# A decoder layer on one core: the residual's moves over six tiles by token half, and the sum with the second half in the later group

## The chip, the core and the metric

The kernel runs on one core of one Trainium2 chip. The metric is the device time of one launch in microseconds (us); lower is better. PE is TensorE, DVE is VectorE, ACT is ScalarE, POOL is GpSimd and SP is SyncE, whose queue issues most transfers. Each engine executes its own queue of instructions in the order in which the built program lists them. That order is not the order of the source: a scheduler in the tile framework sets it at build time, from estimates of its own, under the dependencies between instructions. One changed instruction can so move others, on several engines.

## The reference

One layer: a sparse attention and a causal pooling side by side, a residual and a layer norm, then a gated feed-forward part with a residual and a layer norm. Only the feed-forward part matters here:

```
h = layer_norm(ALPHA * h + mix, ln1_g, ln1_b)          # 272 tokens x 2048; 256 tokens are put out
z = h @ w_up                                           # 2048 -> 2 x 5632
z = sum(zp[:, j:j + T] * conv_w[j] for j in range(3)) + conv_b
a, g = split(z, 2)
f = (gelu(a) * g) @ w_down                             # 5632 -> 2048
h = layer_norm(ALPHA * h + f, ln2_g, ln2_b)
```

## The kernel before

All arithmetic is in float32, and each product is made of three matmuls: every operand is split into a high part (a reduced-precision float32 that PE takes at full rate) and the rest, the low part, and high x high, high x low and low x high are summed.

**Weight tiles.** Every weight tile has 128 x 2048 numbers, 1 MB. `fetch` loads it on SP's queue (L111). Then ScalarE makes the high part, in two cuts of the columns (L124), and VectorE the low part (L125); this is called the conversion below. Three raw tiles and three converted ones can be live at a time. A raw tile's place comes free when its conversion is done, a converted tile's when PE is done with it.

**The feed-forward plan.** `ffn_plan` lists the work by f, the number of a block of 128 inner columns, 0 to 43, in parts of 8. For each f there are two *up tiles*, first half (`za`) and second half (`z`), each of 48 matmuls (L175 to L177, `product`) followed by the convolution of its sum: one operation on ScalarE (L683), two on VectorE (L684, L685). After the second, `gate` does the activation (L700) and the product (L701). Pairs of f are then made into the operands of the down product by `forms`: sums on GpSimd (L720 to L723), splits on ScalarE and VectorE (L706, L707).

For the first four parts the down product is done by a scheme with seven products in place of eight. `seven` works a part's down tiles in two column halves c, and each half in two groups: group A has the products P2, P3, P1, P5 and four tiles, called A j=0 to 3, of 12 matmuls each; group B has P7, P6, P4 and four tiles of 9 matmuls (L745 to L747). The tiles of a part go between the up tiles of the next: up, A, up, A, and so on. The tiles of part 0 stand between the up tiles of f=8 to 15: A j=0 to 3 in f=8 and 9, B j=0 to 3 in f=10 and 11, then the second column half from f=12. Before their conversion the weights of an A tile need one subtraction (L116), those of a B tile three operations (L119 to L121), all on VectorE.

**The result y2.** `y2` holds the residual and the running sum: two token halves i=0 and 1 of 128 tokens, each with 2048 columns. For a column half c, c11 and c12 are pieces of 512 columns in token half 0, c21 and c22 the same in token half 1. At the end of group A ScalarE copies P1 and P5 out as u and v (L757, L759), and VectorE adds P2 to c11, P3 to c12 and v to c22 (`add`, L753). Accumulating transfers on GpSimd's queue then add u to c11 and v to c12 (L763, L764). At the end of group B VectorE makes u += P6 (L767) and v = u + P7 (L768) and adds P4 to c21, and three transfers (L770 to L772) add u to c12 and v to c21 and c22.

**The moves.** The residual enters y2 by 32 transfers on SP's queue (L677, `residual`), each of 32 partitions x 16 x 32 numbers, 64 KB in runs of 128 bytes, one for each of four source blocks a, four destination blocks b and two token halves i. The blocks in place are turned by VectorE at f=4 and 5 (L842). The list `moves` has i as its fastest index, and 8 moves go out after each of f=6, 7, 8 and 9, between the loads of weight tiles. An addition into y2 waits for the moves that write its piece, thus the first ones at the end of group A of f=9.

Of the kernel before, what the change touches and what calls it, by code (L numbers as in the profile page):

```python
# [36 lines left out]
FOLDED = 4  # L37
# [32 lines left out]
def tile_layer(ctx, tc, xt, w_first, w_proj, w_uk, w_uv, w_pool, w_o, w_up, w_down, cols, rows, rel_bias, onehot, out):  # L70
# [8 lines left out]
    def big():  # L79
        return pm.tile([P, 512], F32, tag="mm", name="mm")  # L80

    def small():
        return pa.tile([P, 512], F32, tag="at", name="at")
# [46 lines left out]
    def emit(i):  # L130
        if i in ready:
            return
        if i == last:

            raw = wp.tile([P, 2048], F32, tag="wraw", name="wraw")
            nc.sync.dma_start(raw, stream[i])
            ready[i] = []
            for c in range(0, 2048, 256):
                hl = ring.tile([P, 2, 256], F32R, tag="act", name="whl_r", padded_shape=[P, 2, T])
                nc.scalar.activation(hl[:, 0, :], raw[:, c:c + 256], AF.Copy)  # L140
                nc.vector.tensor_tensor(hl[:, 1, :], raw[:, c:c + 256], hl[:, 0, :].bitcast(F32), op=ALU.subtract)
                ready[i].append(hl)
            return
        if i == spare:
            raw = wp.tile([P, 2048], F32, tag="wraw", name="wraw")
            hl = sb.tile([P, 2, 2048], F32R, tag="y", name="whl_y")
        else:
            raw, hl = weight_tiles()
        fetch(raw, hl, stream[i], kinds.get(i))
        ready[i] = hl  # L150
# [6 lines left out]
    def weights(ahead=2):  # L157
        i = state["use"]
        state["use"] += 1
        prefetch(i + 1 + ahead)  # L160
        return ready.pop(i)
# [7 lines left out]
    def product(ps, hl, m, act, lo, hi, ks=range(KT), width=P, k0=0, k1=KT):  # L169

        for n in range(k0, k1):
            k = ks[n]
            wh, wl = hl[:, 0, k * width:k * width + m], hl[:, 1, k * width:k * width + m]
            ah, al = act[k][:, 0, lo:hi], act[k][:, 1, lo:hi]
            nc.tensor.matmul(ps, wh, ah, start=n == 0, stop=False)  # L175
            nc.tensor.matmul(ps, wh, al, start=False, stop=False)  # L176
            nc.tensor.matmul(ps, wl, ah, start=False, stop=n == KT - 1)  # L177
# [3 lines left out]
    for k0, k1 in [(k, k + 1) for k in range(9)] + [(9, 12), (12, 15), (15, 16)]:  # L181
# [7 lines left out]
        for k in range(k0, k1):  # L189
            xk, wk, c = raw[:, k % 3, :T], raw[:, k % 3, T:], slice(k % 6 * MF, k % 6 * MF + MF)  # L190
            a = ring.tile([P, 2, T], F32R, tag="act", name="xp")
# [84 lines left out]
    v = sb.tile([P, 3], F32, name="rms_v")  # L276
# [103 lines left out]
    for i, (a, b) in enumerate(((0, NM), (NM, NM + P), (NM + P, T))):  # L380
        if i:
            v = ap_.tile([b - a, 1024], F32, name=f"v{i}")
        else:

            v = ap_.tile([80, 1024], F32R, name="v0")
# [290 lines left out]
        to = y2[dst, i, :].rearrange("p (m d) -> p m d", d=P)[:, :, src]  # L676
        nc.sync.dma_start(to, y[src, :, t:t + 32])  # L677

    moves = [(a, b, i) for a in range(4) for b in range(4) for i in range(2)]

    def conv(j, half_, src, za):
        z = fp.tile([P, S], F32, name="z", tag="z1") if half_ else za
# [16 lines left out]
    def gate(za, zg):  # L699
        nc.scalar.activation(za, za, AF.Gelu_apprx_tanh)  # L700
        nc.vector.tensor_tensor(za, za, zg, op=ALU.mult)  # L701

    held = {}
# [30 lines left out]
    def seven(kind, part, c, j):  # L734

        hl = weights()
        n = PARTS[part] // 2
        names = (("P2", 2), ("P3", 3), ("P1", 0), ("P5", 1)) if kind == "A" else (("P7", 1), ("P6", 0), ("P4", 2))
        if j == 0:
            for name, _ in names:  # L740
                held[name] = small()
        for name, w in names:
            a, i = pairs[part][j][name]
            ps, w = held[name], slice(512 * w, 512 * w + 512)
            nc.tensor.matmul(ps, a[:, 0, i], hl[:, 0, w], start=j == 0, stop=False)  # L745
            nc.tensor.matmul(ps, a[:, 0, i], hl[:, 1, w], start=False, stop=False)  # L746
            nc.tensor.matmul(ps, a[:, 1, i], hl[:, 0, w], start=False, stop=j == n - 1)  # L747
        if j < n - 1:
            return
        c11, c12, c21, c22 = (y2[:, i, w:w + 512] for i in range(2) for w in (512 * c, 1024 + 512 * c))  # L750

        def add(to, ps):
            nc.vector.scalar_tensor_tensor(to, to, 1.0 if part else ALPHA, ps, op0=ALU.mult, op1=ALU.add)  # L753

        if kind == "A":
            held["u"] = fp.tile([P, 512], F32, name="u", tag="u1", bufs=1, padded_shape=[P, 2 * NQ])
            nc.scalar.activation(held["u"], held["P1"], AF.Copy)  # L757
            held["v"] = fp.tile([P, 512], F32, name="v", tag="u2", bufs=1, padded_shape=[P, 2 * NQ])
            nc.scalar.activation(held["v"], held["P5"], AF.Copy)  # L759
            add(c11, held["P2"])  # L760
            add(c12, held["P3"])
            add(c22, held["v"])
            nc.gpsimd.dma_start(c11, held["u"], accum_op=ALU.add)  # L763
            nc.gpsimd.dma_start(c12, held["v"], accum_op=ALU.add)  # L764
        else:
            u, v = held["u"], held["v"]
            nc.vector.tensor_tensor(u, u, held["P6"], op=ALU.add)  # L767
            nc.vector.tensor_tensor(v, u, held["P7"], op=ALU.add)  # L768
            add(c21, held["P4"])
            nc.gpsimd.dma_start(c12, u, accum_op=ALU.add)  # L770
            nc.gpsimd.dma_start(c21, v, accum_op=ALU.add)
            nc.gpsimd.dma_start(c22, v, accum_op=ALU.add)  # L772
# [4 lines left out]
    for item in plan:  # L777
        if item[0] in "AB":
            seven(*item)
            continue  # L780
        if item[0] == "down":
            _, part, c, g = item
            hl = weights()
            if g == 0:
                downs = [big(), big()]
            n = PARTS[part]
            for k in range(4 * g, 4 * g + 4):
                w = slice(512 * (k - 4 * g), 512 * (k - 4 * g) + 512)
                for i in range(2):
                    t = slice(i * P, (i + 1) * P)  # L790
                    a = gated[k - n]
                    nc.tensor.matmul(downs[i], a[:, 0, t], hl[:, 0, w], start=k == 0, stop=False)  # L792
                    nc.tensor.matmul(downs[i], a[:, 0, t], hl[:, 1, w], start=False, stop=False)  # L793
                    nc.tensor.matmul(downs[i], a[:, 1, t], hl[:, 0, w], start=False, stop=k == n - 1)  # L794
            if g == n // 4 - 1:
                for i in range(2):
                    yc = y2[:, i, 512 * c:512 * c + 512]
                    nc.vector.tensor_tensor(yc, yc, downs[i], op=ALU.add)
            continue
        _, f, half_ = item  # L800
        part = next(p for p in range(len(PARTS)) if f < sum(PARTS[:p + 1]))
        f0 = sum(PARTS[:part])
        if part == len(PARTS) - 1 and half_ == 0 and f - f0 in (0, 2):
            emit((last, spare)[(f - f0) // 2])
        if half_ == 0:
            if f % 2 == 0:
                pair = fp.tile([P, 2, S], F32, name="za", tag="z0")
            both = []
        hl = weights()
        ps = big()  # L810
        if f < FOLDED:
            k = 0
            if f + half_ == 0:
                product(ps[:, :NE], hl, P, folded, 0, NE, k1=7)
                deviation()
                product(ps[:, :NE], hl, P, folded, 0, NE, k0=7, k1=14)
                deviation_rows()
                k = 14
            product(ps[:, :NE], hl, P, folded, 0, NE, k0=k)
            while len(h_parts) < min(KT, 3 * (2 * f + half_ + 1)):  # L820
                normalise(len(h_parts))
            both.append(ps)
            if half_ == 0:
                continue
            both = [conv(i * FT + f, i, unfold(both[i]), pair[:, f % 2]) for i in range(2)]
        else:
            product(ps[:, :NQ], hl, P, h_parts, 0, NQ)
            both.append(conv(half_ * FT + f, half_, ps, pair[:, f % 2]))
            if half_ == 0:
                continue  # L830
        gate(*both)
        if part >= FAST:
            a = fp.tile([P, 2, NE], F32R, name="gp", tag="gp", bufs=16)
            gated.append(two_parts(a[:, :, :S], both[0]))
        elif f % 2:
            todo.append((part, pair))
        while todo and f + 1 >= FOLDED:
            p, r = todo.pop(0)
            pairs[p].append(forms(r, len(pairs[p])))
        if f in (FOLDED, FOLDED + 1):  # L840
            for m in range(8 * (f - FOLDED), 8 * (f - FOLDED) + 8):
                nc.vector.transpose(y[:, m, NM:], y[:, m, NM:])  # L842
        if FOLDED + 2 <= f < FOLDED + 6:
            for _ in range(8):
                residual(*moves.pop(0))


# [113 lines left out]
```

## Time and profile before

| | us |
|---|---|
| three runs, median (lowest to highest) | 1077.15 (1076.28 to 1078.40) |
| the profiled execution | 1079.12 |
| its span, first to last instruction | 1077.0 |
| PE busy | 1050.5 |
| VectorE busy | 875.3 |
| ScalarE busy | 592.4 |
| GpSimd busy | 179.6 |

The mean granted clock of PE was 0.989 of full speed. In a row of the windows view the columns are the stretch, its length, the busy time and number of instructions of PE, its weight load, DVE, ACT and POOL, then PE's granted clock, the busy share of the DMA engines and GB/s. A row of the timeline has start, duration, engine, line, operation, output and inputs with shapes, the number of merged instructions, and in brackets how long the engine stood idle before and what ended that. A row of the waits has the total, the number and the longest of them. The page's group rows have count, busy time and mean in ns.

### The profile page before, as it was taken

The page shows a single profiled execution, that of the slowest core. Times are in us where ns is not written, and L with a number is a line of the kernel's source. Part 1 is how long each engine was busy: PE and PEld are TensorE (multiplying, and loading weights), DVE is VectorE, ACT ScalarE, POOL GpSimd, SP SyncE. Part 2 cuts the span into 40 slices and gives each one's busy share as a digit, 9 for nine tenths or more (in the row PEclk, how much of TensorE's full clock was granted, in tenths as well). Part 3 has the DMA queues.
Part 4 walks back from the last instruction along what each step waited for, and adds up shares of the span by engine and source line. Part 5 has one row for each costly group of instructions (what it writes and reads, how often), then busy time and mean ns, then how long its engine had stood idle before and what let it go on. Part 6 is the DMA issues. An engine that isn't in the chain of part 4 may idle for free.

```text
span 1077.0 us, 19083 instructions
## 1 busy us (share of the span) xinstructions
PE 1050.5 (98%) x7674; PEld 996.5 (93%) x7674; DVE 875.3 (81%) x1339; ACT 592.4 (55%) x940; POOL 179.6 (17%) x235
## 2 busy tenths in 40 slices
PE   9999999999999999889999999999999999999996
PEld 8998999999999989779999999999999999988995
DVE  6879468758779985598999899989999988976657
ACT  6566446645457664455656555565656565544530
POOL 1100013125454310002120121210212000010000
PEclk9999999999999999889999999999999999999998
DMA  8756543444543578578778787888878878887712
GB/s 316 250 177 226 196 138 127 159 166 161 191 158 118 195 204 246 176 247 271 255 283 293 254 270 260 283 292 277 290 245 271 300 288 268 283 268 258 289 42 79
DMA packets 58024, 244.23 MB, mean 227 GB/s; under 512 B 21542, under 2 KB 21968, under 8 KB 31440
## 3 DMA queue, kind: packets, MB, share of 16 engines
q1 hardware_dynamic: 50480, 227.66, 59.1%
q0 software_dynamic: 6880, 14.30, 7.1%
q8 instruction: 60, 0.98, 0.3%
q10 hardware_dynamic: 576, 1.05, 0.3%
q14 instruction: 28, 0.23, 0.1%
HBM read 228.30 MB, written 2.11 MB: 214 GB/s over the span
## 4 chain that ended last, share of the span: by engine, by line
PE 85%; DVE 8%; DMA 2%; ACT 2%; POOL 1%; issue 1%; SPq 0%; DVEq 0%; ACTq 0%; POOLq 0%
PE mm L175 20%; PE mm L176 20%; PE mm L177 20%; PE at L745 4%; PE at L746 4%; PE at L747 4%; DVE whl L125 3%; PE mm L792 1%; PE mm L793 1%; PE mm L794 1%; DMA wraw<-in_w_up 1%; ACT whl L124 1%; DMA wraw<-in_w_down 1%; DVE hp L670 1%; DVE x L666 1%
## 5 line engine op out<-in xcount | busy, mean ns | idle before, releaser
L125 DVE TENSOR_TENSOR whl<-wraw,whl 128x1024 fp32r<-128x1024 f32 (+1 forms) x408 | 478.3, 1207 | 55.6 <-ACT whl L124 54.0
L124 ACT ACTIVATE whl<-wraw 128x1024 fp32r<-128x1024 f32 (+1 forms) x408 | 396.7, 1016 | 147.8 <-DVE wraw L116 36.0
L175 PE MATMUL mm<-hp,whl 128*128 128x258 f32 x1280 | 365.2, 285 | 2.2 <-ACT whl L124 2.2
L176 PE MATMUL mm<-hp,whl 128*128 128x258 f32 x1280 | 363.1, 284 | 0.0
L177 PE MATMUL mm<-hp,whl 128*128 128x258 f32 x1280 | 362.3, 283 | 0.8 <-DVE whl L125 0.8
L175 PEld LDWEIGHTS mm<-hp,whl 128*128 128x128 f32 x1280 | 242.7, 190 | 5.2 <-ACT whl L124 2.4
L176 PEld LDWEIGHTS mm<-hp,whl 128*128 128x128 f32 x1280 | 244.9, 191 | 2.8
L177 PEld LDWEIGHTS mm<-hp,whl 128*128 128x128 f32 x1280 | 244.3, 191 | 1.0 <-DVE whl L125 1.0
L175 PE MATMUL mm<-xp,whl 128*128 128x256 f32 (+5 forms) x384 | 110.9, 289 | 0.0
L176 PE MATMUL mm<-xp,whl 128*128 128x256 f32 (+5 forms) x384 | 109.5, 285 | 0.0
L177 PE MATMUL mm<-xp,whl 128*128 128x256 f32 (+5 forms) x384 | 108.9, 284 | 0.0
L175 PEld LDWEIGHTS mm<-xp,whl 128*128 128x128 f32 x384 | 72.7, 189 | 0.6
L176 PEld LDWEIGHTS mm<-xp,whl 128*128 128x128 f32 x384 | 72.3, 188 | 0.8 <-issue 0.5
L177 PEld LDWEIGHTS mm<-xp,whl 128*128 128x128 f32 x384 | 72.4, 189 | 0.3 <-DVE whl L125 0.2
L683 ACT ACTIVATE z<-mm,cv 128x256 f32<-128x256 f32 x40 | 22.6, 565 | 86.6 <-PE mm L177 86.6
L745 PE MATMUL at<-whl,gp 128*128 128x512 f32 x160 | 64.5, 405 | 3.9 <-ACT whl L124 3.1
L746 PE MATMUL at<-whl,gp 128*128 128x512 f32 x160 | 64.1, 401 | 0.0
L747 PE MATMUL at<-whl,gp 128*128 128x512 f32 x160 | 63.8, 399 | 0.0
L683 ACT ACTIVATE za<-mm,cv 128x256 f32<-128x256 f32 x40 | 22.5, 563 | 71.8 <-PE mm L177 71.8
L723 POOL TENSOR_TENSOR forms<-za 128x128 f32<-128x128 f32 x16 | 15.2, 951 | 173.7 <-DVE za L701 171.9
L684 DVE SCALAR_TENSOR_TENSOR z<-mm,cv,z 128x256 f32<-128x256 f32 x40 | 19.3, 482 | 27.6 <-ACT z L683 27.6
L745 PEld LDWEIGHTS at<-whl,gp 128*128 128x128 f32 x160 | 30.7, 192 | 10.3 <-ACT whl L124 3.3
(306 smaller groups left out, 1919.0 us busy)
## 6 DMA issues: line engine op xcount, KB each, us to landing
wraw<-in_w_up SPq DMA_DIRECT2D x88, 1024.0 KB, 4.9
wraw<-in_w_down SPq DMA_DIRECT2D x76, 1024.0 KB, 6.0
wraw<-in_w_proj SPq DMA_DIRECT2D x24, 1024.0 KB, 5.0
wraw<-in_w_o SPq DMA_DIRECT2D x16, 1024.0 KB, 4.8
y<-v POOLq DMA_DIRECT2D x24, 256.0 KB, 7.4
y<-u POOLq DMA_DIRECT2D x16, 256.0 KB, 3.5
wraw<-in_w_first SPq DMA_DIRECT2D x9, 304.0 KB, 5.6
x<-in_xt SPq DMA_DIRECT2D x1, 2176.0 KB, 8.6
```

What stands on the lines that cost most here:

```text
L124: nc.scalar.activation(hl[:, 0, c], raw[:, c], AF.Copy)
L125: nc.vector.tensor_tensor(hl[:, 1, c], raw[:, c], hl[:, 0, c].bitcast(F32), op=ALU.subtract)
L175: nc.tensor.matmul(ps, wh, ah, start=n == 0, stop=False)
L176: nc.tensor.matmul(ps, wh, al, start=False, stop=False)
L177: nc.tensor.matmul(ps, wl, ah, start=False, stop=n == KT - 1)
L666: nc.vector.tensor_tensor(yd, yd, m2, op=ALU.add)
L683: nc.scalar.activation(z, src[:, 2:NQ], AF.Identity, bias=col(C_B, j), scale=col(C_W, 3 * j + 2))
L684: nc.vector.scalar_tensor_tensor(z, src[:, 1:NQ - 1], col(C_W, 3 * j + 1), z, op0=ALU.mult, op1=ALU.add)
L723: nc.gpsimd.tensor_tensor(s[:, 3], a11, a21, op=ALU.subtract)
L745: nc.tensor.matmul(ps, a[:, 0, i], hl[:, 0, w], start=j == 0, stop=False)
L746: nc.tensor.matmul(ps, a[:, 0, i], hl[:, 1, w], start=False, stop=False)
L747: nc.tensor.matmul(ps, a[:, 1, i], hl[:, 0, w], start=False, stop=j == n - 1)
```

## The change

The list of moves is sorted by token half first, so that all 16 moves of half 0 go before those of half 1. They go out after f=6 to 11, in numbers of 6, 5, 5, 6, 5 and 5, so those of half 0 after f=6, 7 and 8 and those of half 1 after f=9, 10 and 11. The addition of v to c22, in token half 1, goes from the end of group A to the start of group B's end, where v still holds P5. As the changed kernel has one line less ahead of them, its transfers of group A are L762 and L763, and the moved addition is called at L766.

```
-    moves = [(a, b, i) for a in range(4) for b in range(4) for i in range(2)]
+    moves = [(a, b, i) for i in range(2) for a in range(4) for b in range(4)]
...
             add(c11, held["P2"])
             add(c12, held["P3"])
-            add(c22, held["v"])
             nc.gpsimd.dma_start(c11, held["u"], accum_op=ALU.add)
             nc.gpsimd.dma_start(c12, held["v"], accum_op=ALU.add)
         else:
             u, v = held["u"], held["v"]
+            add(c22, v)
             nc.vector.tensor_tensor(u, u, held["P6"], op=ALU.add)
...
-        if FOLDED + 2 <= f < FOLDED + 6:
-            for _ in range(8):
+        if FOLDED + 2 <= f < FOLDED + 8:
+            for _ in range((6, 5, 5)[f % 3]):
                 residual(*moves.pop(0))
```

More of the change, by code (lines that the diff above doesn't have):

```diff
@@ L677, in residual @@
         nc.sync.dma_start(to, y[src, :, t:t + 32])
-    moves = [(a, b, i) for a in range(4) for b in range(4) for i in range(2)]
+    moves = [(a, b, i) for i in range(2) for a in range(4) for b in range(4)]
     def conv(j, half_, src, za):
@@ L761, in seven @@
             add(c12, held["P3"])
-            add(c22, held["v"])
             nc.gpsimd.dma_start(c11, held["u"], accum_op=ALU.add)
@@ L766, in seven @@
             u, v = held["u"], held["v"]
+            add(c22, v)
             nc.vector.tensor_tensor(u, u, held["P6"], op=ALU.add)
@@ L842, in tile_layer @@
                 nc.vector.transpose(y[:, m, NM:], y[:, m, NM:])
-        if FOLDED + 2 <= f < FOLDED + 6:
-            for _ in range(8):
+        if FOLDED + 2 <= f < FOLDED + 8:
+            for _ in range((6, 5, 5)[f % 3]):
                 residual(*moves.pop(0))
```

## The prediction

> **What bounds the kernel now.** I read the page first, then the waits of PE, then the windows around those waits, then the rows of ScalarE, VectorE, SP and GpSimd inside them.
>
> ```profile
> span 1077.0 us, 19083 instructions
> PE 1050.5 (98%) x7674; PEld 996.5 (93%) x7674; DVE 875.3 (81%) x1339; ACT 592.4 (55%) x940; POOL 179.6 (17%) x235
> ```
>
> ```profile
> PE at L745 <- ACT whl L124: 8.9, 2, 5.8
> PE mm L175 <- ACT whl L124: 2.2, 1, 2.2
> PE mm L177 <- DVE whl L125: 0.8, 1, 0.8
> 436.64 1.22 PE L745 MATMUL at<-whl,gp 128*128 128x512 f32 x2 [3.09 <-ACT whl L124]
> ```
>
> The first fence is the page, the second PE's waits from 370 to 520 and the row of one of them. PE is busy for 98% of the span, so a change gains only where PE stands still or runs at a lower clock. Its largest wait is 8.9 us in two pieces, 3.09 and 5.8, for L124, ScalarE's conversion of a weight tile. The windows show where, and what a piece costs when nothing is late (start of the first matmul to start of the next tile's first):
>
> ```profile
> 380.00:390.00 10.00, 9.87 (x69) 9.88 (x70) 9.72 (x14) 7.64 (x11) 1.31 (x1) 0.83 0.80 232
> 430.00:440.00 10.00, 6.87 (x37) 5.56 (x36) 4.94 (x6) 5.33 (x7) 0.00 (x0) 0.78 0.03 4
> 470.00:1040.00 570.00, 569.20 (x3970) 533.24 (x3968) 495.92 (x670) 325.84 (x445) 70.50 (x90) 1.00 0.79 270
> 427.59:436.64 9.05, 5.96 (x49) 5.76 (x47) 1.58 (x4) 1.98 (x4) 0.09 (x1) 0.95 0.13 51
> 436.64:442.33 5.69, 5.64 (x12) 3.97 (x13) 5.69 (x6) 4.18 (x5) 0.00 (x0) 0.50 0.43 121
> 451.01:462.80 11.79, 5.97 (x50) 5.76 (x48) 6.06 (x13) 4.02 (x10) 2.81 (x4) 0.86 0.64 224
> 462.80:466.86 4.06, 4.02 (x9) 2.72 (x10) 4.06 (x5) 2.36 (x3) 0.00 (x0) 0.55 0.54 115
> 482.64:488.44 5.80, 5.80 (x50) 5.80 (x48) 5.53 (x7) 3.67 (x5) 0.00 (x0) 1.00 0.78 285
> 488.44:490.55 2.11, 2.11 (x12) 1.70 (x11) 1.27 (x3) 1.91 (x3) 0.00 (x0) 1.00 1.00 419
> 522.11:524.92 2.81, 2.81 (x14) 2.26 (x13) 2.78 (x6) 2.53 (x4) 0.00 (x0) 1.00 1.00 399
> ```
>
> An up tile takes 5.80 us, a B tile 2.11, an A tile 2.81. At 427.59 the up tile of f=9, first half, takes 9.05, and the A tile j=2 behind it 5.69 at a granted clock of 0.50: (9.05 - 5.80) + (5.69 - 2.81) = **6.13 us**, stall 1. At 451.01 the up tile of f=10 takes 11.79 and the B tile j=0 behind it 4.06: 5.99 + 1.95 = **7.94 us**, stall 2. From 470 to 1040 PE is busy 569.20 of 570.00 us at clock 1.00: nothing is to be had there. An earlier stall near 377 (the waits of 2.2 and 0.8, then clock 0.83 from 380 to 390) lies ahead of the first queue place that moves.
>
> The cause of both is the order in ScalarE's queue; the last two lines are SP's, with the landing times of all loads from 415 to 450:
>
> ```profile
> 425.01 0.57 ACT L683 ACTIVATE z<-mm,cv 128x256 f32<-128x256 f32 x1 [2.47 <-PE mm L177]
> 433.59 0.56 ACT L683 ACTIVATE za<-mm,cv 128x256 f32<-128x256 f32 x1 [8.01 <-PE mm L177]
> 435.55 4.83 ACT L124 ACTIVATE whl<-wraw 128x1024 fp32r<-128x1024 f32 x5
> 457.01 0.56 ACT L683 ACTIVATE za<-mm,cv 128x256 f32<-128x256 f32 x1 [3.96 <-PE mm L177]
> 461.69 1.58 ACT L124 ACTIVATE whl<-wraw 128x1024 fp32r<-128x1024 f32 x2 [0.96 <-DVE wraw L120]
> ```
>
> ```profile
> 418.27 0.33 SPq L111 DMA_DIRECT2D wraw<-in_w_down  x1
> DMA to landing us min/median/max: 4.7/6.1/9.0
> ```
>
> ScalarE stood idle 8.01 us for PE to finish the up tile (L683 reads its sum), while the conversion that PE needs next was queued behind L683. The raw tile of A j=2 was sent for at 418.27 and landings took 9.0 at most here, so it lay there by 427.3. From 430 to 440 the DMA engines were busy for 0.03: the transfers did not hold PE, the order did. Call this an **inversion**: L683, and VectorE's L684 behind it, ahead of the conversion that PE wants right after.
>
> **The change, part by part.** What it does to the queues I read from the two built programs, instruction by instruction; PE gets its tiles in the same order in both.
>
> *Stalls 1 and 2 go: -14.07 us.* In the changed program the four L124 of A j=2 and of the next up tile stand ahead of the L683 of f=9, and the L124 of B j=0 ahead of the L683 of f=10. I give the two stalls back whole, 6.13 + 7.94.
>
> *Price B, a new inversion: +6.1 us.* The moves now run on to f=11, and in ScalarE's queue the two L683 of f=10 second half and f=11 first half stand next to each other; the L124 of B j=2 follows, on VectorE L119 to L121 too. This is stall 2 one pair of tiles later, without the three additions that stood in it:
>
> ```profile
> 457.61 0.48 DVE L684 SCALAR_TENSOR_TENSOR za<-mm,cv,za 128x256 f32<-128x256 f32 x1 [4.08 <-ACT za L683]
> 458.01 1.27 DVE L753 SCALAR_TENSOR_TENSOR y<-y,at 128x512 f32<-128x512 f32 x2
> 459.20 0.69 DVE L753 SCALAR_TENSOR_TENSOR y<-y,v 128x512 f32<-128x512 f32 x1
> 459.80 0.48 DVE L685 SCALAR_TENSOR_TENSOR za<-mm,cv,za 128x256 f32<-128x256 f32 x1
> ```
>
> The chain is L683, L684, L119, L685, L120, L124, PE. The three L753 took 458.01 to 459.89, 1.88 us, so the price is 7.94 - 1.88 = 6.06. Bounds: the stall near 377 has 3.0 us of idle time and (1 - 0.83) x 10 = 1.7 us of lost clock, 4.7 in all; stall 2 whole is 7.94.
>
> *Price A, B j=0 a little late: +1.0 us.* Its L124 now stands behind the copies u and v (L757, L759) and the forms (L706) of the pair just gated, and GpSimd's queue has both accumulating transfers among the forms. The same passage one group later in the trace:
>
> ```profile
> 524.42 0.60 ACT L757 ACTIVATE u<-at 128x512 f32<-128x512 f32 x1
> 525.32 0.87 POOL L763 DMA_DIRECT2D y<-u  x1 [12.93 <-ACT u L757]
> 526.01 0.83 POOL L720 TENSOR_TENSOR forms<-za 128x128 f32<-128x128 f32 x1
> 526.93 0.46 POOL L721 TENSOR_TENSOR forms<-forms,za 128x128 f32<-128x128 f32 x1
> 527.47 0.52 POOL L722 TENSOR_TENSOR forms<-za,forms 128x128 f32<-128x128 f32 x1
> 528.02 0.42 ACT L706 ACTIVATE gp<-forms 128x256 fp32r<-128x256 f32 x1 [1.05 <-POOL forms L722]
> 528.85 1.04 ACT L124 ACTIVATE whl<-wraw 128x1024 fp32r<-128x1024 f32 x1
> ```
>
> Count from the start of A j=3 (522.11 there). Transfer of u at 3.2, L720 at 3.9, the transfer of v at 4.8 (0.69 ahead of the next, as from 525.32 to 526.01), L721 at 5.5, L722 from 6.0 to 6.5, two L706 to 7.1, L124 to 8.2. VectorE does three L707 (0.4 apart) and L121 from 7.0, then its L125 (1.2 by the row below) from 8.6 to 9.8. PE wants B j=0 at 2.81 + 5.80 = 8.6, has the high part at 8.2, but its second matmul, at 8.8, needs the low part: 1.0 late. Bounds: 0, and 2.7 should the clock drop too (1.7 as near 377).
>
> *Price C, A j=0 of the second column half: +2.4 us.* The moves of f=11 now stand ahead of its load on SP, and its L116 has gone from ahead of the gate to behind the whole end of group B on VectorE:
>
> ```profile
> L125 DVE TENSOR_TENSOR whl<-wraw,whl 128x1024 fp32r<-128x1024 f32 (+1 forms) x408 | 478.3, 1207 | 55.6 <-ACT whl L124 54.0
> 495.71 0.68 DVE L767 TENSOR_TENSOR u<-u,at 128x512 f32<-128x512 f32 x1
> 496.31 0.68 DVE L753 SCALAR_TENSOR_TENSOR y<-y,at 128x512 f32<-128x512 f32 x1
> 496.90 0.68 DVE L768 TENSOR_TENSOR v<-u,at 128x512 f32<-128x512 f32 x1
> ```
>
> Count from the end of the up tile of f=11, second half. L683 to 0.6; VectorE, held by L125 to 1.1, does L684, L767, L685 and the gate to 3.1. On GpSimd L720 starts at 3.3 and L722 ends at 5.3 to 5.9; L706 and L707 of it end at 6.2 to 6.8. Then four operations 0.6 apart: the sum with the second half (moved here), L753, L768, L116, to 8.7 to 9.3. L124's first cut follows to 9.8 to 10.4, L125 to 11.0 to 11.6. PE wants the tile at 2.11 + 5.80 = 7.9, does two matmuls of the other cut and waits; the tile ends 1.5 to 2.0 late, and the next up tile's low part another 0.7: 2.4. Bounds: 0; 4.1 with a clock drop.
>
> Stall 1, an idle gap of 3.09 us, was followed by a tile at clock 0.50, and near 377 gaps of 2.2 and 0.8 were followed by 0.83. The Trainium skill (TensorE: Matmul & The Clock Gate, HAM oscillation — how this bites in real kernels) gives as its rule that PE should have no idle gaps over about 3.4 us, since those throttle it. The trace disagrees at 3.09 us, and the measurement decides. By the rule neither A nor C costs clock and the sum below stands; by the row near 377 a drop would add 1.7.
>
> *The moves: 0.* There are 32 before and after, on the same queue and engines:
>
> ```profile
> 439.39 7.51 SPq L677 DMA_DIRECT2D y<-x  x8
> DMA to landing us min/median/max: 2.2/5.3/7.0
> ```
>
> Eight took 7.51 us of SP's queue, so five take 4.7. They now stand ahead of the loads of B j=0, B j=2 and that A j=0. Cover: raw tiles lie waiting for their conversion. B j=2's load goes out after five moves, which start when B j=0 is converted, so some 3.5 us into the up tile of f=10, second half; PE wants it 2.3 + 2.11 + 5.80 = 10.2 later, and no load took over 9.0. Without the cover each costs up to 4.7.
>
> *The sum with the second half: 0 in the other seven groups.* It goes three places back in VectorE's queue, 0.69 us each, under the busy PE of 470 to 1040. In the first group it waits for the last moves; behind it stand L753, L768, L116 and C's tile. The last four moves follow the load of f=12, which goes when B j=2 is converted, about 2 us after that tile starts (462.80 and two L124 in stall 2), so 8 us before the end of the up tile behind it (4.06 + 5.80 - 2). They are out 4 us later and landed 7.0 after that at most, 3 us past that end; the sum's turn comes at 6.2 to 6.8. No cost.
>
> *Sum:* -14.07 + 6.1 + 1.0 + 2.4 = **-4.6 us**. The profiled execution took 1079.12 us with its span of 1077.0, so 1074.5; it lies 1.97 above the median of the runs shown, 1077.15. Taken from that median: **1072.6 us**.
>
> **The rivals.**
> *Only B is left (0.20).* GpSimd's spans are rough, so A and C may be hidden: -14.07 + 6.1 = -8.0, 1069.2. For it: no PE wait of this size from 470 to 1040. Against it: there, L116 and the first L124 stood ahead of the forms.
> *C drops the clock, or A does (0.25).* 1.7 more: 1074.3; both, 1076.0. For it: the waits near 377, 2.2 and 0.8 us, did it. Against it: C's idle time is under 2 us.
> *The transfers were the cause (0.08).* If moves ahead of weights held PE, spreading them holds PE in more places: five moves, 4.7 us, at B j=0 and at A j=0 on top of B give -14.07 + 6.1 + 9.4 = +1.4, about 1078.6, no change. Against it: the DMA share of 0.03 in stall 1.
> *The sum with the second half blocks VectorE (0.07), the slower end.* Place: its turn, 6.8 us after f=11's second up tile. If the last moves land 4 us after that turn, C grows from 2.4 to 6.4 and drops the clock, 2.9 as in the tile at 0.50 (5.69 - 2.81): -14.07 + 6.1 + 1.0 + 6.4 + 2.9 = +2.3, 1079.5. Slower from these 4 us on. For it: the moves lie behind weight loads in the same queue. Against it: a landing of about 15 us, where 7.0 was the most.
>
> **How the numbers follow.** Forecast 0.40 (1071 to 1074), and 0.20, 0.25, 0.08, 0.07 in the order above. The range: low end -14.07 + 4.7 = -9.4, 1067.7; high end -14.07 + 7.94 + 2.7 + 4.1 = +0.7, 1077.8. A measurement of this kernel tells about 0.2%, 2.15 us, from no change: faster is under 1075.0. That is 0.40 + 0.20 + 0.15 of the clock rival = 0.75; within: 0.10 + 0.08 = 0.18; slower 0.07.
>
> **What would show it.** Right: no PE wait near 433; up tiles of 5.80 through f=10; one wait of about 3.9 us ahead of B j=2 with a clock near 0.5 behind it; a wait under 2 us at the next A j=0. Wrong: a PE wait for a DMA, VectorE's moved addition waiting for a move, or B absent. If B j=2's tile lands late, or C runs at half clock, my zero for the moves or my C is what failed.

## The result and the profile after

The changed kernel took **1073.78 us**, the median of six runs (1073.11 to 1074.38), beside 1077.88 for six runs of the kernel before (1076.28 to 1079.14). The ratio is 0.9963, with a 95% interval from 0.9950 to 0.9976: 4.1 us faster, where 4.6 had been forecast. The profiled run has a span of 1071.0 us at a mean granted clock of 0.993. The page shows what did not change: the work.

```profile
span 1071.0 us, 19086 instructions
PE 1046.4 (98%) x7674; PEld 992.8 (93%) x7674; DVE 876.1 (82%) x1339; ACT 593.0 (55%) x940; POOL 181.7 (17%) x235
```

The next view is PE's waits from 370 to 520 us, the stretch read in the prediction. Each row has the total, how many waits, and the longest.

```profile
PE at L745 <- ACT whl L124: 5.1, 2, 3.9
PE mm L175 <- ACT whl L124: 2.2, 1, 2.2
PE at L746 <- DVE whl L125: 1.5, 2, 1.1
PE mm L177 <- DVE whl L125: 1.2, 2, 0.8
```

The 8.9 us of L745 in two waits has become 5.1, again in two. But they are not what is left of the old ones. The rows of PE's timeline for L745 and L746, from 440 to 500, put each in its place:

```profile
451.60 0.50 PE L746 MATMUL at<-whl,right 128*128 128x512 f32 x1 [1.08 <-DVE whl L125]
471.30 0.87 PE L745 MATMUL at<-whl,right 128*128 128x512 f32 x2 [3.90 <-ACT whl L124]
472.56 0.79 PE L746 MATMUL at<-whl,right 128*128 128x512 f32 x1 [0.39 <-DVE whl L125]
490.97 0.73 PE L745 MATMUL at<-whl,gp 128*128 128x512 f32 x2 [1.18 <-ACT whl L124]
```

The first is B j=0 (term A of the prediction), the two in the middle are B j=2 (term B), the last is A j=0 of the second column half (term C). With the waits of 2.2 and 0.8 near 378 and one of 0.48 at 494.28 these are all; there is none between 417 and 450, where stall 1 lay. What each place costs is read from the windows of the tiles, from the start of one tile's first matmul to the start of the next tile's; the columns are those of the prediction's windows.

```profile
426.75:432.56 5.81, 5.81 (x50) 5.81 (x49) 4.81 (x6) 2.01 (x2) 1.31 (x1) 1.00 0.66 203
443.94:450.01 6.07, 5.96 (x49) 5.75 (x47) 3.97 (x9) 2.99 (x7) 3.93 (x5) 1.00 0.50 88
450.01:453.55 3.54, 2.45 (x10) 1.80 (x10) 3.54 (x5) 2.98 (x4) 0.00 (x0) 1.00 0.23 32
461.45:471.30 9.85, 5.95 (x50) 5.74 (x48) 4.32 (x10) 2.09 (x4) 0.46 (x1) 1.00 0.66 266
471.30:475.47 4.17, 3.78 (x10) 2.63 (x11) 4.17 (x5) 2.36 (x3) 0.00 (x0) 0.59 0.32 65
489.17:493.40 4.23, 3.05 (x14) 2.18 (x13) 4.19 (x7) 3.53 (x5) 1.77 (x2) 1.00 0.71 121
493.40:499.94 6.54, 6.06 (x49) 5.85 (x48) 6.17 (x7) 4.20 (x5) 0.00 (x0) 1.00 1.03 353
```

The first row is the up tile of f=9, first half, which took 9.05 and takes 5.81. The pairs behind it are A, B and C. Against the undisturbed lengths of 5.80, 2.11 and 2.81:

| place | first tile | second tile | cost, us | predicted |
|---|---|---|---|---|
| stalls 1 and 2 of before | at their normal length | A j=2 2.79; B j=0 is in A | -14.07 | -14.07 |
| A, ahead of B j=0 | 6.07 - 5.80 | 3.54 - 2.11 | +1.70 | +1.0 |
| B, ahead of B j=2 | 9.85 - 5.80 | 4.17 - 2.11 | +6.11 | +6.1 |
| C, A j=0 of the second half | 4.23 - 2.81 | 6.54 - 5.80 | +2.16 | +2.4 |
| sum | | | -4.10 | -4.6 |

That this sum equals the difference of the medians, 4.10, to the second digit is chance: the interval of the ratio alone is 1.4 us to either side. The spans of the two profiles differ by 6.0 us and not by 4.1. Of the other 1.9, 0.83 lies ahead of all this: the first A tile, j=0, starts at 415.37 instead of 416.20, and PE's wait of 2.2 near 377 is as much earlier. Another 1.1 lies near 630, where PE waited 0.8 us for VectorE's L767 in the profile of before; no other profile here has that wait.

How the new order looks in ScalarE's queue is shown by its timeline, first at the place of the old stall 1, then at the new one:

```profile
424.64 2.00 ACT L124 ACTIVATE whl<-wraw 128x1024 fp32r<-128x1024 f32 x2
427.00 2.01 ACT L124 ACTIVATE whl<-wraw 128x1024 fp32r<-128x1024 f32 x2 [0.35 <-ACT whl L124]
432.76 0.57 ACT L683 ACTIVATE za<-mm,cv 128x256 f32<-128x256 f32 x1 [3.75 <-PE mm L177]
433.22 2.00 ACT L124 ACTIVATE whl<-wraw 128x1024 fp32r<-128x1024 f32 x2
...
467.44 0.56 ACT L683 ACTIVATE za<-mm,cv 128x256 f32<-128x256 f32 x1 [7.02 <-PE mm L177]
470.19 3.47 ACT L124 ACTIVATE whl<-wraw 128x1024 fp32r<-128x1024 f32 x4 [0.23 <-DVE wraw L120]
```

At 432.76 ScalarE waits for PE's up tile, as before, but the conversions of the two tiles that PE wants next, A j=2 (from 424.64) and the up tile behind it (from 427.00), were done ahead of that wait. So the wait costs nothing. At 467.44 it waits 7.02 us with the conversion of B j=2 behind it, and PE stands until 471.30.

### The profile page after: what moved, and what is told of

Same layout as the page of the kernel before. It is cut to its first block, busy times and chain, and to the rows that moved or that the text cites. A ratio compares the mean times of both kernels' runs of the same rounds, so it can differ in the third digit from the quotient of the medians.

```text
span 1071.0 us, 19086 instructions
## 1 busy us (share of the span) xinstructions
PE 1046.4 (98%) x7674; PEld 992.8 (93%) x7674; DVE 876.1 (82%) x1339; ACT 593.0 (55%) x940; POOL 181.7 (17%) x235
## 3 DMA queue, kind: packets, MB, share of 16 engines
HBM read 228.30 MB, written 2.11 MB: 215 GB/s over the span
## 4 chain that ended last, share of the span: by engine, by line
PE 88%; DVE 7%; POOL 1%; ACT 1%; DMA 1%; issue 1%; SPq 0%; DVEq 0%; ACTq 0%; POOLq 0%
PE mm L175 21%; PE mm L176 21%; PE mm L177 20%; PE at L745 5%; PE at L746 5%; PE at L747 5%; DVE whl L125 2%; PE mm L792 1%; PE mm L793 1%; PE mm L794 1%; DVE hp L670 1%; DVE x L666 1%; ACT whl L124 1%; DMA wraw<-in_w_up 1%; PE mm L238 1%
## 5 line engine op out<-in xcount | busy, mean ns | idle before, releaser
L125 DVE TENSOR_TENSOR whl<-wraw,whl 128x1024 fp32r<-128x1024 f32 (+1 forms) x408 | 478.9, 1208 | 50.6 <-ACT whl L124 47.9
L124 ACT ACTIVATE whl<-wraw 128x1024 fp32r<-128x1024 f32 (+1 forms) x408 | 397.3, 1017 | 131.5 <-DVE wraw L116 27.5
L683 ACT ACTIVATE z<-mm,cv 128x256 f32<-128x256 f32 x40 | 22.6, 564 | 91.5 <-PE mm L177 91.5
L745 PE MATMUL at<-whl,gp 128*128 128x512 f32 x160 | 63.3, 398 | 1.2 <-ACT whl L124 1.2
L746 PE MATMUL at<-whl,gp 128*128 128x512 f32 x160 | 63.1, 395 | 0.0
L747 PE MATMUL at<-whl,gp 128*128 128x512 f32 x160 | 62.9, 393 | 0.0
L683 ACT ACTIVATE za<-mm,cv 128x256 f32<-128x256 f32 x40 | 22.5, 563 | 72.6 <-PE mm L177 72.6
L723 POOL TENSOR_TENSOR forms<-za 128x128 f32<-128x128 f32 x16 | 15.8, 986 | 173.4 <-DVE za L701 171.6
```

Source lines behind the costliest of these rows:

```text
L124: nc.scalar.activation(hl[:, 0, c], raw[:, c], AF.Copy)
L125: nc.vector.tensor_tensor(hl[:, 1, c], raw[:, c], hl[:, 0, c].bitcast(F32), op=ALU.subtract)
L683: nc.scalar.activation(z, src[:, 2:NQ], AF.Identity, bias=col(C_B, j), scale=col(C_W, 3 * j + 2))
L723: nc.gpsimd.tensor_tensor(s[:, 3], a11, a21, op=ALU.subtract)
```

## The experiments

Theory: the time is set by the inversions alone, that is by whether L683, which waits for PE, stands ahead of a conversion that PE needs next. The change alters the time by altering where the scheduler puts them. Rivals: the transfers themselves (their bytes or their time on a queue); the token order; the moved sum. In the kernels with a pin, helper lines shift the numbers: there L125 and L126 are the conversion (L124 and L125 of before), L687 is L683, L749 and L750 are L745 and L746. In e7, L112 is the load, L679 a move and L680 its twin, and L117 and L120 are L116 and L119. The expectations speak of these things under the names of the prediction.

### Two order edges, no other change (e1)

In the kernel before, two operations of the convolution, those of f=9 and f=10 (first half), are put behind the high part of the tile that PE takes next. All 32 moves and all sums stay as they were.

```
-            nc.scalar.activation(hl[:, 0, c], raw[:, c], AF.Copy)
+            state["high"] = nc.scalar.activation(hl[:, 0, c], raw[:, c], AF.Copy)
...
+        high[i] = state["high"]
...
-        nc.scalar.activation(z, src[:, 2:NQ], AF.Identity, bias=col(C_B, j), scale=col(C_W, 3 * j + 2))
+        behind = tc.issue_after(high[state["use"]].ins) if (j % FT, half_) in ((9, 0), (10, 0)) else ExitStack()
+        with behind:
+            nc.scalar.activation(z, src[:, 2:NQ], AF.Identity, bias=col(C_B, j), scale=col(C_W, 3 * j + 2))
```

> The kernel before with its moves as they were (8 after each of f=6 to 9, halves mixed, the sum in group A); only two operations are pinned: ScalarE's L683 of the up tile of f=9, first half, and that of f=10, first half, may not be issued ahead of the conversion (L124) of the down tile that PE wants next. Theory of the order: both stalls go, 14.07 us in the trace, and B j=0 is left late by 1.0 to 1.7 as in price A, so about 1065 us against 1077.9, faster than the changed kernel (1073.8) although not one transfer is changed. Rival, the transfers hold PE: the weights still arrive behind eight moves, so about 1077 to 1078.

Measured: 1064.43 us (1063.49 to 1067.90) beside 1077.64, ratio 0.9882, interval 0.9865 to 0.9898. PE's waits from 417 to 520:

```profile
PE at L749 <- ACT whl L125: 0.9, 1, 0.9
PE at L750 <- DVE whl L126: 0.5, 1, 0.5
```

Of 8.9 us of waits for the conversion 0.9 is left. Same bytes, same queue, same places between the loads, and 13.2 us less: the transfers did not hold PE in the kernel before, the order did. It gains three times what the change gains.

### The moved sum alone (e2)

```
             add(c12, held["P3"])
-            add(c22, held["v"])
...
             u, v = held["u"], held["v"]
+            add(c22, v)
```

> The kernel before with the sum with the second half moved to group B alone, the moves as before. Theory of the order: ScalarE's queue keeps both inversions, and stall 2 loses one 0.6 us operation of its chain, so 1077.3 us against 1077.9. Rival, the sum is a gain of its own: 1076 or less.

Measured: 1077.64 us beside 1077.64, ratio 1.0002, interval 0.9993 to 1.0012. It does not even leave the place it should leave. VectorE's timeline ahead of B j=0 in this kernel:

```profile
457.82 0.68 DVE L753 SCALAR_TENSOR_TENSOR y<-y,v 128x512 f32<-128x512 f32 x1
458.42 0.68 DVE L119 TENSOR_TENSOR wraw<-wraw 128x512 f32<-128x512 f32 x1
```

The addition of v is later in the source, but the scheduler put it again directly ahead of L119, in the chain that PE waits for. The wait of L745 is 8.9 us in both kernels.

### The token order and the sum, but still eight moves over four tiles (e3)

```
-    moves = [(a, b, i) for a in range(4) for b in range(4) for i in range(2)]
+    moves = [(a, b, i) for i in range(2) for a in range(4) for b in range(4)]
```

with the edit of e2. (The spread without the moved sum cannot be tried: that sum needs moves of half 1, which then have not been sent.)

> The moves by token half as in the changed kernel and the sum in group B, but 8 after each of f=6 to 9 as before. Theory of the order: the two inversions are still in ScalarE's queue, so 1077.3 us, and the whole gain lies in the spreading over six tiles. Rival, the gain lies in the token order (the additions of half 0 wait for fewer moves): about 1074 as in the changed kernel.

Measured: 1076.86 us beside 1077.64, ratio 0.9994, interval 0.9985 to 1.0003. PE's waits over the whole span:

```profile
PE at L745 <- ACT whl L124: 7.8, 2, 4.8
```

Both inversions are there; the second is 1.0 shorter, since two additions left its chain. So the token order and the moved sum are not what gains: with them given, the spread over six tiles is what lets the scheduler place the conversions differently. The order of ScalarE's instructions in the built programs says it in a line each (C is L683 with its f and a or b for the half, w one cut of L124, g the activation, u and v the copies, t L706):

```
before  C8b C9a g wwwwwwww C9b uvtttt C10a g wwwwwwww C10b wwww C11a w g www C11b
after   C8b wwww C9a ww g ww C9b uvtttt wwww C10a g wwww C10b C11a g wwwwwwww C11b
e1      C8b ww C9a ww g wwww C9b uvtttt ww C10a ww g wwww C10b wwww C11a g wwww C11b
e3      C8b C9a g wwwwwwww C9b uvtttt C10a g wwwwwwww C10b wwww C11a
```

Two C with no w between them are an inversion: C8b C9a and C9b ... C10a before, C10b C11a after.

### The change with its own inversion taken out (e4)

The change, with e1's pin at f=11 and f=12 in place of 9 and 10.

> The changed kernel with ScalarE's L683 of f=11 and of f=12, first halves, pinned behind the conversion of the next down tile, nothing else. Theory: price B goes (6.11 us in the trace), A (1.70) and C (2.16) stay, so 1073.8 - 6.1 = 1067.7 us. Rival, B is the five moves ahead of B j=2's load: no change, 1073.8.

Measured: 1068.90 us (1067.77 to 1070.74) beside 1077.64, ratio 0.9919, interval 0.9905 to 0.9932. B falls from 6.11 to 1.0 (B j=2 2.60, the next up tile 6.30), A stays at 1.7, and C grows from 2.16 to 3.16. PE's row at C and the window behind it:

```profile
485.64 0.73 PE L749 MATMUL at<-whl,gp 128*128 128x512 f32 x2 [2.17 <-ACT whl L125]
```

```profile
485.64:490.00 4.36, 3.88 (x20) 3.23 (x21) 4.32 (x6) 3.55 (x5) 0.32 (x1) 1.00 1.07 230
```

So term B is that one inversion: without it 5.1 us come back, 1.0 is lost again at C, and the gain over the kernel before is 8.7 us in place of 4.1. C grew because VectorE was still converting B j=3 (4.10 us from 473.26) when the second half of f=11 ended at 474.94.

### The moves on GpSimd's queue (e5)

```
-        nc.sync.dma_start(to, y[src, :, t:t + 32])
+        nc.gpsimd.dma_start(to, y[src, :, t:t + 32])
```

in the kernel before; order and numbers of the moves unchanged.

> The kernel before with the 32 moves issued from GpSimd's queue in place of SP's, same number, bytes and tiles (8 after each of f=6 to 9), sum in group A. In the built program no L683 stands ahead of a conversion that PE wants next, and L124 of B j=0 and A j=0 stand ahead of the forms. Theory of the order: stalls 1 and 2 go and neither A, B nor C comes: 1077.6 - 14.07 = 1063.6 us, perhaps 1 to 2 more if GpSimd's issuing (0.9 us each) delays the forms. Rival, the transfers hold PE: same bytes on the same 16 DMA engines, so about 1077 us.

Measured: **1063.90 us** (1062.22 to 1065.49) beside 1078.63, ratio 0.9862, interval 0.9845 to 0.9879: the lowest median here, though its interval overlaps that of e1. PE has no wait at all from 417 to 520. With no move between the loads on SP, the scheduler puts conversions ahead of every L683 in question, without a pin. The same 64 KB transfers still run; they landed in 7.5 us at the median, where they took 5.3 from SP. So their bytes are excluded a second time; their time on SP's queue is not tested here, since it is gone too, and only e1 excludes that.

### The moves on ScalarE's queue (e6)

The same line with `nc.scalar`.

> The same with the moves issued from ScalarE's queue. The order of L683 and L124 is without an inversion here too. Theory: both stalls go, but if each move holds ScalarE as it held SP (7.51 us for eight) conversions wait behind moves: 1064 to 1072 us. Rival, the transfers hold PE: about 1077 us.

Measured: 1072.90 us beside 1078.63, ratio 0.9948, interval 0.9934 to 0.9963: just above the range expected. No wait of L745 for L124 is left on PE, but the moves now stand in the queue that the conversions stand in. ScalarE's timeline:

```profile
426.81 5.71 ACTq L677 DMA_DIRECT2D y<-x  x6
432.62 3.90 ACT L124 ACTIVATE whl<-wraw 128x1024 fp32r<-128x1024 f32 x4 [5.25 <-DMA y<-x]
...
452.16 1.58 ACT L124 ACTIVATE whl<-wraw 128x1024 fp32r<-128x1024 f32 x2 [1.08 <-issue]
453.64 0.58 ACT L757 ACTIVATE u<-at 128x512 f32<-128x512 f32 x1
```

Six moves held the conversions for 5.25 us. Further on, L124 and the copy u came late, and PE waited 1.8 us for u. Four tiles from 417 to 500 are late by 5.9 us in all, of the 6.5 by which the span of this profile exceeds that of e5.

### The order of e1 with twice the transfers (e7)

e1, and behind each move a second one of the same form into a scratch in DRAM that nothing reads. Only transfers are added.

```
         nc.sync.dma_start(to, y[src, :, t:t + 32])
+        nc.sync.dma_start(twin[16 * i + 4 * a + b], y[src, :, t:t + 32])
```

> The order-only kernel (before, two L683 pinned) in which every move is followed by a second transfer of the same 64 KB to a scratch array that nothing reads, so 64 small transfers for 32, still on SP. Theory: the order keeps PE fed as long as the loads behind the moves land before their conversion's turn; sixteen moves take about 15 us of SP, 7.5 more than before, and the cover of B j=0's load is about as long, so 1064 to 1069 us. Rival, the transfers held PE in the kernel before: doubling them costs at least what the stalls cost, 1077 us or more.

Measured: 1077.77 us beside 1078.63, ratio 0.9997, interval 0.9987 to 1.0007. The theory's range was missed and the rival's number came true: the whole gain of e1 is gone. But it does not follow that the moves held PE in the kernel before, which e1 excludes; twice as many hold it. The waits of ScalarE and VectorE from 410 to 470 say why; e1 has no such row there:

```profile
ACT whl L125 <- DMA wraw<-in_w_down: 7.4, 1, 7.4
DVE wraw L117 <- DMA wraw<-in_w_down: 5.8, 1, 5.8
DVE wraw L120 <- DMA wraw<-in_w_down: 2.7, 1, 2.7
```

SP's timeline has the cause. A load goes out at 440.60, the next at 453.56; between them the queue does nothing but moves and their twins:

```profile
440.60 0.33 SPq L112 DMA_DIRECT2D wraw<-in_w_up  x1
440.98 0.60 SPq L679 DMA_DIRECT2D y<-x  x1
...
452.83 0.63 SPq L680 DMA_DIRECT2D twin<-x  x1
453.56 0.56 SPq L112 DMA_DIRECT2D wraw<-in_w_down  x1
```

The tile of B j=0 lands at 459.52 and PE stands for it until 462.13. So "moves: 0" of the prediction is no property of the moves. The raw tiles that lie waiting cover the 7.8 us of moves that stand there on SP in e1, and not these 12.5. Seven tiles from 416 to 467 are late by 13.7 us in all.

### The moves over all twelve up tiles (e8)

The change, with two or three moves behind each up tile of f=6 to 11 instead of five or six behind each second one.

```
+                if FOLDED + 2 <= f < FOLDED + 8:
+                    for _ in range((3, 2, 3)[f % 3]):
+                        residual(*moves.pop(0))
                 continue
...
-            for _ in range((6, 5, 5)[f % 3]):
+            for _ in range((3, 3, 2)[f % 3]):
```

> The changed kernel with its moves spread more finely: 2 or 3 after each of the twelve up tiles of f=6 to 11. The two L683 of f=10 and f=11 are no longer neighbours in ScalarE's queue; B j=0 and the next A j=0 still stand behind the forms. Theory: price B (6.11 us in the trace) goes, A (1.70) and C (2.16, perhaps 3.2) stay: 1073.8 - 6.1 = 1067.7, up to 1069 us. Rival, B is the moves ahead of the loads: there are as many, so 1073 to 1074 us.

Measured: 1075.19 us beside 1078.63, ratio 0.9967, interval 0.9955 to 0.9979: the same gain as the change, not more. A miss, and the reading of the built order was wrong: the two cuts ahead of L683 of f=11 belong to the up tile, not to B j=2. One inversion became two smaller ones, as ScalarE's timeline shows:

```profile
470.95 0.56 ACT L683 ACTIVATE za<-mm,cv 128x256 f32<-128x256 f32 x1 [6.23 <-PE mm L177]
471.41 1.05 ACT L124 ACTIVATE whl<-wraw 128x1024 fp32r<-128x1024 f32 x1
...
481.80 0.56 ACT L683 ACTIVATE z<-mm,cv 128x256 f32<-128x256 f32 x1 [6.30 <-PE mm L177]
482.27 1.04 ACT L124 ACTIVATE whl<-wraw 128x1024 fp32r<-128x1024 f32 x1
```

The tiles here are late by 1.7 us at A, by 3.6 at B j=2 with the up tile ahead of it, and by 5.0 at B j=3 with the up tile ahead of it and the two behind it: 10.3 in all, beside 9.97 in the changed kernel.

### Term A: the transfer of v behind the forms (e9)

```
-            nc.gpsimd.dma_start(c12, held["v"], accum_op=ALU.add)
+            with tc.issue_after(held["form"].ins):
+                nc.gpsimd.dma_start(c12, held["v"], accum_op=ALU.add)
```

where `held["form"]` is the operation of L722. GpSimd in the changed kernel, ahead of B j=0:

```profile
445.46 1.46 POOL L763 DMA_DIRECT2D y<-v  x1
446.18 1.64 POOL L721 TENSOR_TENSOR forms<-forms,za 128x128 f32<-128x128 f32 x1
447.89 0.47 POOL L722 TENSOR_TENSOR forms<-za,forms 128x128 f32<-128x128 f32 x1
```

> The changed kernel with one difference: GpSimd issues the accumulating transfer of v at the end of each group A only behind the operation of the forms that L721 and L722 belong to; the queues of the other engines are as in the changed kernel. Theory A1 (the transfer's own time on GpSimd is what stretched L721 from 0.46 to 1.64 us): L721 ahead of B j=0 takes about 0.5 us, L722 ends about 1.1 us earlier, and the two late tiles of term A shrink from 1.70 us to about 0.6; the time about 1 us under that of the changed kernel, 1072.8. Theory A2 (VectorE's L119 and L120, which ran beside it and took 0.93 and 0.83 us where 0.68 is usual, held it): L721 stays above 1.2 us and term A at about 1.7; the time 1073.8. B (6.1) and C (2.2) stay in both.

Measured: 1075.96 us beside 1078.37, ratio 0.9976, interval 0.9961 to 0.9991: the gain over the change that theory A1 expected is not there. The median lies above A2's 1073.8 too, but the change's interval, 0.9950 to 0.9976, overlaps this one, so that e9 is slower than the change is not shown. GpSimd's and PE's rows there:

```profile
447.89 0.80 POOL L721 TENSOR_TENSOR forms<-forms,za 128x128 f32<-128x128 f32 x1
448.76 0.47 POOL L722 TENSOR_TENSOR forms<-za,forms 128x128 f32<-128x128 f32 x1
```

```profile
452.47 0.51 PE L745 MATMUL at<-whl,right 128*128 128x512 f32 x1 [0.85 <-ACT whl L124]
453.73 0.80 PE L746 MATMUL at<-whl,right 128*128 128x512 f32 x1 [0.75 <-DVE whl L125]
```

L721 falls from 1.64 to 0.80. That alone does not decide for A1, since the other queues did not stay as they were, which the expectation had taken for granted: the scheduler put L120 behind the three L707 on VectorE, so of L119 and L120 only L119 still runs beside L721. The changed kernel has rows in which VectorE works beside GpSimd and GpSimd issues no transfer:

```profile
427.43 1.31 POOL L723 TENSOR_TENSOR forms<-za 128x128 f32<-128x128 f32 x1 [11.93 <-DVE za L701]
427.20 3.75 DVE L125 TENSOR_TENSOR whl<-wraw,whl 128x1024 fp32r<-128x1024 f32 x3
```

In all eleven profiles the 120 operations of the forms with neither VectorE nor a transfer beside them took 0.45 to 0.47 us. L720, just ahead of L721, took 1.03 in both kernels with L707 and L119 beside it, though transfers overlapped it for 0.91 us in the changed kernel and 0.28 here. So VectorE alone stretches such an operation, without any transfer, and A1 is not shown. What share of the 1.64 the transfer has stays open: e9 took L120 and the transfer away from L721 together, and no run has L119 and L120 beside the whole of it without the transfer. In e8 an L723 with parts of both beside it, and no transfer, took 0.78.

Term A did not shrink. The first cut of L124, which follows L120, began 8.5 us after the start of A j=3, where it was 7.8 in the changed kernel. PE waited twice, and in this profile the clock fell as well:

```profile
452.47:457.25 4.78, 4.03 (x10) 2.99 (x10) 4.78 (x6) 2.82 (x4) 0.00 (x0) 0.64 0.38 101
```

Of its ten executions five took 1072.86 to 1074.46 us with mean clocks of 0.992 to 0.994, and five 1077.45 to 1078.18 with 0.989. The profile is of one of the second five; its A j=0 starts 1.7 us later than in the profile of the changed kernel, which is ahead of everything that e9 changes.

## Why the prediction was right

**The two stalls go: right.** Both tiles behind them have their normal length, and e1 shows that order alone takes them away. e5 shows the same without a pin, and e4 shows it for the new inversion of term B.

**Price B, 6.1: right,** 6.11 measured, with a gap of 3.90 and a clock of 0.59 in the tile behind. It came from stall 2 less the three additions, so the price of an inversion could be read from one that was already in the trace. e4 takes it out and gets 5.1 of it back. That the size agrees to 0.05 is in part luck: in e9 the same gap of 3.90 cost 7.0 (tiles of 9.85, 4.41 and 6.49 us), because the clock was at 0.50 for 6.83 us behind it and not for 3.41.

**Price A, 1.0: mechanism right, mis-sized,** 1.70 measured. The step that failed is L721 at 0.46 us, taken from a row beside which GpSimd issued nothing and VectorE did L753 and L707. Here L119, L120 and a transfer ran beside it, and it took 1.64 (the rows of e9 do not separate them), and L722 ended 7.2 us after the start of A j=3 where the count had 6.5. The 0.7 is the whole miss of term A. In the trace of before L723 took 0.46 to 1.31 us, the longest ones beside L125 and without a transfer: a warning that the time of such an operation depends on what VectorE does meanwhile.

**Price C, 2.4: right** in mechanism and nearly in size: 2.16, of which 0.74 in the next up tile, where 0.7 was counted.

**No clock drop at A and C: right in the profile of the changed kernel,** where the windows of both show 1.00, but this is in part luck. In e9, A's gaps of 0.85 and 0.75 had a tile at 0.64 behind them; in e4 C's gap of 2.17 had 1.00. The Trainium skill (TensorE: Matmul & The Clock Gate, HAM oscillation — how this bites in real kernels) bars gaps over about 3.4 us; the 3.90 at B agrees, the 0.85 and 0.75 in e9 do not. The last section has what the traces show of it.

**The moves, 0: right for 32, by a margin that has an end.** e1 and e7 put the end between 7.8 and 12.5 us of moves between two loads.

**The moved sum, 0: right.** VectorE's timeline in the changed kernel has it at its turn with no wait in brackets, so it did not wait for the last moves:

```profile
487.35 0.69 DVE L753 SCALAR_TENSOR_TENSOR y<-y,v 128x512 f32<-128x512 f32 x1
```

The rival that this sum blocks VectorE is refuted by this row, the rival that the transfers were the cause by e1 and e5, the rival that only B is left by the measured A and C.

The forecast gain was 0.5 us too large; A's 0.7 and C's -0.2 are that difference.

## What to carry to other kernels

When the busiest engine waits for a conversion that was ready to run, look at what stands ahead of it in the in-order queue, not at the transfers; an operation that waits for the busy engine itself must not stand ahead of work that this engine needs next. A change that seems to be about transfers may act only through the order that a scheduler derives from them, and then it moves the stall as readily as it removes it: compare the built queues, and try an order edge or two, which here gained three times as much (0.9882), or take the small transfers off the queue that carries the loads (0.9862). A cover is a quantity: measure how much of it is left before calling a step free.

## What the runs showed of the hardware

- The granted clock fell after gaps far shorter than 3 us in some executions and not after longer ones in others. Near 377 all eleven profiles have the same wait of 2.2 us on PE, with 0.8 (in e9 0.5) behind it. The windows from 380 to 390, first of the changed kernel, then of e4, have clocks of 0.85 and 1.00:

```profile
380.00:390.00 10.00, 10.00 (x74) 10.00 (x74) 9.72 (x15) 7.04 (x10) 1.48 (x2) 0.85 0.89 273
```

```profile
380.00:390.00 10.00, 10.00 (x85) 10.00 (x84) 9.89 (x15) 7.33 (x10) 1.52 (x2) 1.00 0.85 263
```

  The traces keep the record of the granted clock. From 370 to 500 us it has two values, 1.00 and 0.50; every stretch at 0.50 is one, two or three times 3.41 us long, and the stretches at 1.00 between them are whole multiples of 3.41 too, so the clock changes on a grid. At the gaps near 377, e2 and e4 have no stretch at 0.50, six profiles have one of 3.41 us, and e5, e6 and e9 have two in a row. From the end of the second gap to the start of A j=0 they took 34.6, 35.9 to 36.1, and 36.9 to 37.2 us: so 3.41 us at 0.50 cost about 1.5 us here, and twice that about 2.5. The outcome sorts by the place of the first gap on the grid: two where it began 0.72 to 1.49 us behind a grid point, none at 1.54 and 1.83, one at 2.28 to 3.09 and at 0.30. Whether a short gap costs clock is so not settled by its length alone. Its place on a grid, which differs from execution to execution, goes with it; by what rule is not shown.
- An operation of GpSimd on 128x128 numbers took 0.45 to 0.47 us with nothing beside it, 1.31 with VectorE's L125 beside it (L723), and 1.64 with L119, L120 and the issue of a transfer beside it (L721).
- Issuing from ScalarE cost what issuing from GpSimd did not: 1072.90 against 1063.90 us for the same 32 transfers, since ScalarE's queue held the conversions.
